# Hybrid SSD and attention block on one core: down-phase pools on other operands' places, output half by token tiles, meta keys of 128 rows

## The chip, the cores and the metric

One core of a Trainium2 chip. The metric is device time in microseconds for one execution of the whole kernel. The kernel before took 2267.64 us (median of three runs, 2267.42 to 2267.79).

## What is computed

One decoder layer over 1024 tokens of 1024 features, with 16 learned meta tokens ahead of them (L = 1040) which are dropped at the output. The reference, cut to what matters here:

```python
u = rms_norm(h, norm_mix_w)
z, xbc, dt, c_q, c_kv, k_rope, g_ssm, g_mla = split(u @ w_in)
y_ssm = ssd_mixer(...)                  # Mamba-2, chunks of 128
y_mla = mla_mixer(...)                  # 8 heads, causal, keys include the 16 meta tokens
    p = softmax(where(mask, s, -inf))
    o = einsum("bhqk,bkhv->bqhv", p, v)
mixed = sigmoid(g_ssm) * (y_ssm @ w_branch_ssm) + sigmoid(g_mla) * (y_mla @ w_branch_mla)
h = h + mixed @ w_out
v = rms_norm(h, norm_mlp_w)
h = h + square(relu(v @ w_mlp_up)) @ w_mlp_down
return rms_norm(h, final_norm_w)[:, 16:]
```

## The kernel before

Everything is float32. Each product is made of three matmuls on split operands: ACT casts a value to its high part (L69 from SBUF, L112 from PSUM), DVE subtracts that from the value to get the low part (L70, L113), and `mm` (L100) runs high x high, high x low and low x high. Weights come in units of 128 x 1024 (512 KB) by SP's DMA queue into tiles `st`, and their splits are the tiles `w`. Token tiles are 128 rows; the meta tokens are a ninth tile of 16 (`TILES` in the code, T and off being a tile's length and place). A scheduler with a simulated timeline sets the order of the instructions of each engine; the kernel text gives the dependences. SBUF pools are stacked from the left or the right side, so a pool that is opened later lies where closed ones lay, and its tiles wait for the last use of what lay there.

The program in the order of time: normalisation, transposes and the small key and dt projections (`pb`, L222 ff., `keys_and_dt`) for the nine token tiles; projections, convolution, gates and the SSD scan to 924 us; attention to 1254; branch products `pbr` and the output projection `pout` in two halves of 512 tokens to 1587; norms and transposes `tpv` to 1612; the MLP's up product to 1925 and its down product to 2252; the final norm.

Attention goes by head h (8) and block b of 256 queries. `probabilities` makes one 128-query row tile of softmaxed scores `pr`; `weighted_values` transposes them on PE (`pp`, L737), splits them into `pT` (L112, L113), and multiplies with the values `vt` to `po` (L100). Keys are taken in groups: first the 16 meta keys alone (kt = -1), then pairs of 128-key tiles. For the meta keys `pT` and `vt` have 16 rows, so each (h, b) issues three `po` of 16 rows, 96 in all; the other 480 have 128. `vt` holds nine key tiles for two heads (`values`, products `pv`), built once per head pair.

`out_half(t, mixed)` (L855 ff.) takes the two 512-column halves c of `w_out` one after the other; in each, all four token tiles' PSUM banks are filled in parallel over the eight k tiles, and only then DVE adds `pout` to `res` (L877). `row_norm` (L903 ff.) of a token tile needs both halves: squares on ACT (L911), their sum on DVE (L912), the power on POOL (L120), two scalings on DVE (L915). The up phase needs, for tokens 512 to 1023, `B22` and the four differences `T1` to `T4` (L941 to L947), each transposed on PE (`tpv`) and split; `B11` and `B21` come from the first half.

The MLP's two products each save an eighth of the block products (seven in place of eight per 2 x 2 block). Up: for each g of 8, seven products of 24 matmuls with `xT` or `xB` tiles (`xop`), from g = 1 on in the order B11, T1, T2, B22, T3, B21, T4; the hidden blocks go to DRAM (`d_h`, POOL's queue). Down: for each kb of 4, seven products of 48 matmuls from `h` (reloaded by `hid` as `hr` on SP's queue, L1091) and `w` (from `w_down`, slots `sd`, L963). Their results are added into the tiles `acc` (L1115), which POOL's queue has loaded from `d_res` (L1074, sixteen of 256 KB). `t1` is b12 - b11 first (L1119). In the profile `pm<-w,h` are the down matmuls, and the last product of each kb is the one of bank set `F`. After the last, `finish_row` runs `row_norm` per token tile and writes `out` (L1084).

## Time and profile before

| | us |
|---|---|
| median of three runs | 2267.64 |
| the profiled execution | 2268.88 |
| its span, first to last instruction | 2266.4 |
| PE busy | 2207.6 |
| DVE busy | 1371.3 |
| ACT busy | 1016.4 |
| POOL busy | 295.4 |

PE is TensorE's matmuls, PEld its weight loads, which run beside matmuls; DVE is VectorE, ACT ScalarE, POOL GpSimd, SP SyncE. A group's busy time counts overlapping instructions once. Where a row has "[x <-engine tile]", the engine sat idle x us before it, until that work was done. The mean granted TensorE clock of the span is 0.990 of full speed.

### The profile page before, as it was taken

To read this page: it belongs to the slowest core of one execution; us is meant where nothing else is said; L and a number is where in the kernel's file an instruction comes from. 1 tells how busy PE (TensorE), PEld (TensorE's weight loads), DVE (VectorE), ACT (ScalarE), POOL (GpSimd) and SP (SyncE) were. 2 spreads that over 40 slices of the span, in tenths; PEclk is the share of its full clock that TensorE was granted. 3 is DMA by queue.
4 is the path that set the end of the run, shared out by engine and by line. 5 is a ranking of instruction groups with operands and counts; after the bars stand their busy time and mean duration, and the time that the engine had idled before them with its cause. 6 is when DMAs were issued, how large, how long until landed. Compare 5 with 4: busy or idle time off the path is not lost.

```text
span 2266.4 us, 31520 instructions
## 1 busy us (share of the span) xinstructions
PE 2207.6 (97%) x12294; PEld 1934.0 (85%) x12294; DVE 1371.3 (61%) x2062; ACT 1016.4 (45%) x1824; POOL 295.4 (13%) x398
## 2 busy tenths in 40 slices
PE   7999999999999999999999999999899999699997
PEld 7999998999989988898888888888688887588886
DVE  6632468769769686356555333335764644777776
ACT  4432255646546454466665222232554545333333
POOL 2100002102112022000002121011021212100000
PEclk9999999999999999999999999999899999899999
DMA  6443454625526446522118686344344534854442
GB/s 191 103 99 89 103 147 131 149 62 162 126 85 159 97 139 160 200 57 64 54 47 256 204 278 223 111 126 135 102 164 134 172 116 154 292 167 140 149 121 84
DMA packets 238260, 314.57 MB, mean 139 GB/s; under 512 B 18576, under 2 KB 172048, under 8 KB 237600
## 3 DMA queue, kind: packets, MB, share of 16 engines
q1 hardware_dynamic: 148816, 201.31, 28.9%
q0 software_dynamic: 89296, 111.26, 17.8%
q8 instruction: 96, 1.57, 0.3%
q14 instruction: 52, 0.43, 0.1%
HBM read 221.11 MB, written 91.41 MB: 138 GB/s over the span
## 4 chain that ended last, share of the span: by engine, by line
PE 94%; DMA 3%; DVE 2%; ACT 1%; issue 1%; SPq 0%; POOL 0%; DVEq 0%; POOLq 0%; ACTq 0%
PE pm L100 26%; PE pg L100 16%; PE px L100 12%; PE pbr L100 11%; PE po L100 4%; PE pq L100 4%; PE pout L100 4%; PE sc L100 4%; PE pd L569 2%; PE pp L737 2%; PE pb L100 1%; PE pv L100 1%; DMA st<-in_w_down 1%; PE ps L100 1%; PE pr L100 1%; PE pk L100 1%
## 5 line engine op out<-in xcount | busy, mean ns | idle before, releaser
L70 DVE TENSOR_TENSOR w<-st,w 128x1024 fp32r<-128x1024 f32 x194 | 245.5, 1266 | 267.4 <-ACT w L69 266.4
L100 PE MATMUL pm<-w,h 128*128 128x512 f32 x1344 | 307.4, 391 | 19.4 <-ACT h L69 16.6
L100 PEld LDWEIGHTS pm<-w,h 128*128 128x128 f32 x1344 | 253.6, 189 | 73.2 <-ACT h L69 17.1
L69 ACT CAST w<-st 128x1024 fp32r<-128x1024 f32 x194 | 203.5, 1050 | 227.1 <-PE pbr L100 140.7
L100 PE MATMUL px<-uT,w 128*128 128x346 f32 (+1 forms) x1728 | 290.7, 323 | 0.0
L100 PEld LDWEIGHTS px<-uT,w 128*128 128x128 f32 x1728 | 275.6, 188 | 1.5
L100 PE MATMUL pbr<-ring,w 128*128 128x512 f32 x1152 | 264.8, 391 | 0.0
L100 PEld LDWEIGHTS pbr<-ring,w 128*128 128x128 f32 x1152 | 215.7, 188 | 45.9
L100 PE MATMUL pg<-w,uT 128*128 128x256 f32 x1536 | 195.8, 283 | 0.0
L100 PE MATMUL pg<-uT,w 128*128 128x512 f32 x768 | 194.3, 400 | 0.0
L100 PEld LDWEIGHTS pg<-w,uT 128*128 128x128 f32 x1536 | 188.1, 188 | 2.1 <-issue 0.4
L100 PE MATMUL pm<-xT,w 128*128 128x512 f32 x768 | 183.3, 395 | 0.0
L100 PEld LDWEIGHTS pm<-xT,w 128*128 128x128 f32 x768 | 144.0, 187 | 35.0
L100 PEld LDWEIGHTS pg<-uT,w 128*128 128x128 f32 x768 | 140.9, 188 | 30.7
L69 ACT CAST h<-hr 128x1024 fp32r<-128x1024 f32 x56 | 58.9, 1054 | 183.3 <-PE pm L100 172.2
L100 PE MATMUL pm<-xB,w 128*128 128x512 f32 x576 | 138.2, 396 | 1.6 <-ACT w L69 1.6
L100 PEld LDWEIGHTS pm<-xB,w 128*128 128x128 f32 x576 | 109.1, 190 | 26.9 <-ACT w L69 1.9
L419 DVE SCALAR_TENSOR_TENSOR xs<-raw,cw,xs 128x1040 f32<-128x1040 f32 x72 | 93.1, 1298 | 8.7 <-ACT xs L417 7.9
L511 ACT ACTIVATE m<-m,nacs 128x128 f32<-128x128 f32 x256 | 78.9, 390 | 39.5 <-DMA m<-d_acs 39.4
L100 PE MATMUL po<-pT,vt 128*128 128x256 f32 (+2 forms) x576 | 93.7, 291 | 1.6 <-ACT pT L112 0.7
L70 DVE TENSOR_TENSOR h<-hr,h 128x1024 fp32r<-128x1024 f32 x56 | 68.2, 1221 | 42.1 <-ACT h L69 42.1
L100 PE MATMUL pout<-w,mix 128*128 128x512 f32 x384 | 90.9, 396 | 0.0
(259 smaller groups left out, 3374.1 us busy)
## 6 DMA issues: line engine op xcount, KB each, us to landing
st<-in_w_in SPq DMA_DIRECT2D x60, 512.0 KB, 4.2
hr<-d_h SPq DMA_DIRECT2D x56, 512.0 KB, 3.6
m<-d_acs SPq DMA_DIRECT2D x32, 512.0 KB, 4.3
d_y<-yT POOLq DMA_DIRECT2D x32, 512.0 KB, 5.0
st<-in_w_bs SPq DMA_DIRECT2D x32, 512.0 KB, 3.6
ring<-d_y POOLq DMA_DIRECT2D x16, 1024.0 KB, 14.1
st<-in_w_up SPq DMA_DIRECT2D x32, 512.0 KB, 3.9
d_h<-hs POOLq DMA_DIRECT2D x64, 256.0 KB, 3.2
```

The source lines that it names most:

```text
L69: act.copy(out=hi, in_=src)
L70: dve.tensor_tensor(out=lo, in0=src, in1=f(hi), op=ALU.subtract)
L100: pe.matmul(out=out, lhsT=l, rhs=r, start=start, stop=stop, skip_group_check=more)
L419: dve.scalar_tensor_tensor(out=xs, in0=raw[:, k : k + L], scalar=cw[:, ct, k : k + 1], in1=xs, op0=ALU.mult, op1=ALU.add)
L511: act.activation(out=m[:, h, :], in_=m[:, h, :], func=AF.Relu, bias=nacs[:, i, hh])
L569: pe.matmul(out=pd[:, cs], lhsT=q["m"][:, h, :], rhs=q["xd"][:, cs], start=True, stop=True)
L737: pe.transpose(out=pt[:T, n : n + P], in_=prs[i - 2 * b][0][:, c0 : c0 + T], identity=ident)
```

## The change

1. `keys_and_dt`: the meta tile's products take 128 token columns as the stationary operand in place of 16 (the further ones belong to the next token tile and are not used).
2. Attention: the meta keys' `pT` becomes one of two permanent tiles `pTm` of 128 rows, zeroed once; slot 0 of `vt` is zeroed by POOL for each head pair, and the three `po` of the meta keys take all 128 rows.
3. The second output half becomes `out_rows`: token tiles outside, c inside; all eight units of `w_out` are held, those of c = 1 in a new pool `wop`.
4. `xop` is laid out in another order, and the down phase's pools move: `whl2` (for `h`) first and on the left, `sd` and `sh` on the right. `acc` becomes eight tiles of 128 x 1024, loaded by eight DMAs of 512 KB on POOL after the first product has been written down; `frow` comes there too.
5. The last product of the last kb runs by token tiles (`by_rows`); each `finish_row` writes one 512 KB output, on SP's queue for even and on ACT's for odd tiles.

```diff
@@ -224,10 +224,10 @@
             T, off = TILES[i]
             pb = pc.tile([P, 512], F32, tag="c", name="pb")
             for k in range(KD):
-                uh, ul = (uT[:, j, k, off : off + T] for j in (0, 1))
+                uh, ul = (uT[:, j, k, off : off + P] for j in (0, 1))
                 for w, us in ((0, uh), (1, uh), (0, ul)):
                     first, last = k == 0 and us is uh and w == 0, k == KD - 1 and us is ul
-                    mm(pb[:T, :352], us, t1w[:, k, w, :], first, last)
+                    mm(pb[:, :352], us, t1w[:, k, w, :], first, last)
             dve.tensor_copy(out=krr[:T, i, :], in_=pb[:T, 256:320])
             dve.tensor_tensor(out=dtr[:T, i, :], in0=pb[:T, 320:352], in1=dtb[:T], op=ALU.add)
             ckn = ap2.tile([P, 256], F32, tag="ckn", name="ckn", bufs=2)
@@ -636,6 +636,10 @@
         ckv = a0.tile([P, 2, 2, L], F32R, name="ckv")
         kr = a1.tile([P, 2, L], F32R, name="kr")
         causal = a1.tile([P, L], F32, name="causal")
+
+        metas = [a1.tile([P, 2, 256], F32R, name=f"pTm{j}") for j in range(2)]
+        for m in metas:
+            pool.memset(f(m), 0.0)
         pool.dma_start(out=cq, in_=d_cq)
         pool.dma_start(out=ckv, in_=d_ckv)
         pool.dma_start(out=kr, in_=d_kr)
@@ -650,6 +654,7 @@
         def values(wu, hh):
 
             vt = a1.tile([P, 2, 9, 2 * DV], F32R, tag="vt", name="vt")
+            pool.memset(f(vt[:, :, 0, :]), 0.0)
             for i, (T, off) in enumerate(TILES):
                 ps = pbank("pv")
                 out = ps[:T, : 2 * DV]
@@ -719,11 +724,11 @@
 
             out = pso.tile([P, 256], F32, tag="o", name="po")
             vs = slice(DV * hv, DV * (hv + 1))
-            def accumulate(T, pT, pieces):
+            def accumulate(pT, pieces):
                 for z, x in ((0, 0), (1, 0), (0, 1)):
                     for kt, p0, q0 in pieces:
-                        v = vt[:T, z, kt + 1, vs]
-                        mm(out[:, q0:], v, pT[:T, x, p0 : p0 + 256 - q0], kt < 0 and z == x, x == 1 and kt == 2 * b + 1)
+                        v = vt[:, z, kt + 1, vs]
+                        mm(out[:, q0:], v, pT[:, x, p0 : p0 + 256 - q0], kt < 0 and z == x, x == 1 and kt == 2 * b + 1)
 
             ready = []
             for g in [[-1]] + [[kt, kt + 1] for kt in range(0, 2 * b + 2, 2)]:
@@ -736,9 +741,9 @@
                     for i in range(i0, 2 * b + 2):
                         pe.transpose(out=pt[:T, n : n + P], in_=prs[i - 2 * b][0][:, c0 : c0 + T], identity=ident)
                         n += P
-                pT = a2.tile([P, 2, 512], F32R, tag="pT", name="pT", bufs=5)
+                pT = a2.tile([P, 2, 512], F32R, tag="pT", name="pT", bufs=5) if T == P else metas[b % 2]
                 split_psum(pT[:T, 0, :n], pT[:T, 1, :n], pt[:T, :n])
-                ready.append((T, pT, pieces))
+                ready.append((pT, pieces))
                 if len(ready) > PT_AHEAD:
                     accumulate(*ready.pop(0))
                 yield
@@ -876,6 +881,24 @@
                 sp.dma_start(out=dst, in_=a["x"][P * ti : P * (ti + 1), cs])
                 dve.tensor_tensor(out=dst, in0=dst, in1=ps[i], op=ALU.add)
 
+    def out_rows(t, mixed, pl):
+
+        wu = [[wunit(a["w_out"][2 * P * u : 2 * P * (u + 1), 512 * c : 512 * (c + 1)].rearrange("(k p) c -> p k c", p=P),
+                     (2, 512), (whl, pl)[c]) for u in range(4)] for c in range(2)]
+        for i in range(4):
+            ts = slice(P * i, P * (i + 1))
+            for c in range(2):
+                ps = pf.tile([P, 512], F32, tag="f", name="pout")
+                for k in range(8):
+                    wh, wl = (w[:, k % 2, :] for w in wu[c][k // 2])
+                    mm(ps, mixed[k][:, 0, ts], wh, k == 0, False)
+                    mm(ps, mixed[k][:, 0, ts], wl, False, False)
+                    mm(ps, mixed[k][:, 1, ts], wh, False, k == 7)
+                ti = 4 * t + i
+                dst = res[ti][c]
+                sp.dma_start(out=dst, in_=a["x"][P * ti : P * (ti + 1), 512 * c : 512 * (c + 1)])
+                dve.tensor_tensor(out=dst, in0=dst, in1=ps, op=ALU.add)
+
     out_half(0, mix_half(0))
     mixed = mix_half(1)
     ring_stack.close()
@@ -927,12 +950,13 @@
         row_norm(ep, i, row, True)
         transposed(xop["B11"], res[i][0], i)
         transposed(xop["B21"], res[i][1], i)
-    out_half(1, mixed)
+    with ExitStack() as ws:
+        out_rows(1, mixed, ws.enter_context(tc.tile_pool(name="wop", bufs=4, reuse_waits="tile")))
     br.close()
     with tc.using_default_side("right"):
         xb = ctx.enter_context(ExitStack())
         xbp = xb.enter_context(tc.tile_pool(name="xb", bufs=1, reuse_waits="tile"))
-    xop |= {n: xbp.tile([P, 2, 4, 512], F32R, name=f"x{n}") for n in ("B22", "T1", "T3", "T2", "T4")}
+    xop |= {n: xbp.tile([P, 2, 4, 512], F32R, name=f"x{n}") for n in ("T1", "T2", "B22", "T3", "T4")}
     for j in range(4):
         row_norm(ep, 4 + j, row, True)
         (b11, b21), (b12, b22) = res[j], res[4 + j]
@@ -1061,17 +1085,15 @@
     xb.close()
     xa_stack.close()
 
+    whl2 = ctx.enter_context(tc.tile_pool(name="whl2", bufs=4, reuse_waits="tile"))
     dn = ctx.enter_context(tc.tile_pool(name="dn", bufs=1, reuse_waits="tile"))
-    whl2 = ctx.enter_context(tc.tile_pool(name="whl2", bufs=4, reuse_waits="tile"))
-    sd = ctx.enter_context(tc.tile_pool(name="sd", bufs=10, reuse_waits="tile"))
-    sh = ctx.enter_context(tc.tile_pool(name="sh", bufs=4, reuse_waits="tile"))
     ef = ctx.enter_context(tc.tile_pool(name="ef", bufs=2, reuse_waits="tile"))
+    with tc.using_default_side("right"):
+        sd = ctx.enter_context(tc.tile_pool(name="sd", bufs=10, reuse_waits="tile"))
+        sh = ctx.enter_context(tc.tile_pool(name="sh", bufs=4, reuse_waits="tile"))
     row = dn.tile([P, D], F32, name="frow")
-    sp.dma_start(out=row, in_=a["fin_w"].partition_broadcast(P))
-    res = [[dn.tile([P, 512], F32, name=f"acc{i}{c}") for c in range(2)] for i in range(NT)]
-    for i in range(NT):
-        for c in range(2):
-            pool.dma_start(out=res[i][c], in_=d_res[:, i, 512 * c : 512 * (c + 1)])
+    acc = [dn.tile([P, D], F32, name=f"acc{i}") for i in range(NT)]
+    res = [[t[:, 512 * c : 512 * (c + 1)] for c in range(2)] for t in acc]
 
     def split_h(src):
         w = whl2.tile([P, 2, 1024], F32R, tag="w2", name="h")
@@ -1080,8 +1102,7 @@
 
     def finish_row(i):
         row_norm(ef, i, row, False)
-        for c in range(2):
-            sp.dma_start(out=a["out"][P * i : P * (i + 1), 512 * c : 512 * (c + 1)], in_=res[i][c])
+        (sp, act)[i % 2].dma_start(out=a["out"][P * i : P * (i + 1), :], in_=acc[i])
 
     for kb in range(4):
         subs = (2 * kb, 2 * kb + 1)
@@ -1097,17 +1118,27 @@
                 for g in subs
             ]
 
-        def product(out, n, w, start):
+        def product(out, n, w, start, by_rows=False):
+            hs, ws = [], []
+
+            def part(s, i):
+                ts = slice(P * i, P * (i + 1))
+                for k in range(2):
+                    hh, hl = hs[s][:, 0, k, ts], hs[s][:, 1, k, ts]
+                    mm(out[i], hh, ws[s][:, 0, k, :], start and s == k == 0, False, True)
+                    mm(out[i], hh, ws[s][:, 1, k, :], False, False, True)
+                    mm(out[i], hl, ws[s][:, 0, k, :], False, s == k == 1, True)
+
             for s, g in enumerate(subs):
-                hv = split_h(hid(n, g)).rearrange("p j (k c) -> p j k c", k=2)
-                wv = split_unit(w[s]).rearrange("p j (k c) -> p j k c", k=2)
-                for i, o in enumerate(out):
-                    ts = slice(P * i, P * (i + 1))
-                    for k in range(2):
-                        hh, hl = hv[:, 0, k, ts], hv[:, 1, k, ts]
-                        mm(o, hh, wv[:, 0, k, :], start and s == k == 0, False, True)
-                        mm(o, hh, wv[:, 1, k, :], False, False, True)
-                        mm(o, hl, wv[:, 0, k, :], False, s == k == 1, True)
+                hs.append(split_h(hid(n, g)).rearrange("p j (k c) -> p j k c", k=2))
+                ws.append(split_unit(w[s]).rearrange("p j (k c) -> p j k c", k=2))
+                if not by_rows:
+                    for i in range(4):
+                        part(s, i)
+            if by_rows:
+                for i in range(4):
+                    for s in range(2):
+                        part(s, i)
 
         def gather(src, half, c):
             for i, s in enumerate(src):
@@ -1123,6 +1154,10 @@
         combine(t1, b12, b11)
         E, G, F = ([bank() for _ in range(4)] for _ in range(3))
         product(G, 3, t1, True)
+        if kb == 0:
+            sp.dma_start(out=row, in_=a["fin_w"].partition_broadcast(P))
+            for i in (4, 5, 6, 7, 0, 1, 2, 3):
+                pool.dma_start(out=acc[i], in_=d_res[:, i, :])
         gather(G, 1, 1)
         b22 = rows(1, 1)
         product(G, 6, b22, False)
@@ -1139,7 +1174,7 @@
         combine(t1, b21, t1)
         product(E, 1, t1, False)
         gather(E, 1, 0)
-        product(F, 2, b21, True)
+        product(F, 2, b21, True, kb == 3)
         gather(F, 0, 0)
     for i in (4, 5, 6, 7, 0, 1, 2, 3):
         finish_row(i)
```

The rows below are from the built programs: line, operation, output<-inputs, shape, count. ACT from the last two copies of the up phase on, before (`t` is the difference t1; `w<-st` here are casts of w_down):

```order
L1006 ACTIVATE c_17479<-pm 128x512
L1007 ACTIVATE c_17479<-c_17479 128x512
L69 CAST w<-t_17575 128x1024
L69 CAST w<-t_17576 128x1024
L69 CAST w<-st 128x1024 x2
L69 CAST h<-hr 128x1024 x5
L69 CAST w<-st 128x1024
L69 CAST h<-hr 128x1024
L69 CAST w<-st 128x1024
L69 CAST h<-hr 128x1024
```

ACT at the same place now:

```order
L1030 ACTIVATE c_17459<-pm 128x512
L1031 ACTIVATE c_17459<-c_17459 128x512
L69 CAST w<-t_17530 128x1024
L69 CAST w<-t_17531 128x1024
L69 CAST h<-hr 128x1024 x4
L69 CAST w<-st 128x1024 x4
L69 CAST h<-hr 128x1024 x3
L69 CAST w<-t_17530 128x1024
L69 CAST h<-hr 128x1024
L69 CAST w<-t_17531 128x1024
```

Two `w<-st` stood between the casts of `t` and the first `h`; now four `h` come first and four `w<-st` behind them.

SP at the change from up to down, before:

```order
L1070 DMA frow<-in_fin_w 128x1024
L963 DMA st<-in_w_down 128x2x512 x4
L1091 DMA hr<-d_h 128x1024 x4
L963 DMA st<-in_w_down 128x2x512 x6
L1091 DMA hr<-d_h 128x1024 x5
L963 DMA st<-in_w_down 128x2x512
L1091 DMA hr<-d_h 128x1024
L963 DMA st<-in_w_down 128x2x512
```

and now:

```order
L987 DMA st<-in_w_down 128x2x512 x4
L1112 DMA hr<-d_h 128x1024 x4
L987 DMA st<-in_w_down 128x2x512 x4
L1112 DMA hr<-d_h 128x1024 x3
L1158 DMA frow<-in_fin_w 128x1024
L1112 DMA hr<-d_h 128x1024
L987 DMA st<-in_w_down 128x2x512 x4
L1112 DMA hr<-d_h 128x1024 x7
```

The first twelve loads are in the same order; `frow`, which stood ahead of all, now stands behind fifteen.

DVE from the add of the last `pout` on, before (`res_14719` is tile 3's second half; `res_14714` to `res_14717` are tiles 1 and 2, and another 35 rows follow up to the first `w<-st`):

```order
L877 TENSOR_TENSOR res_14719<-res_14719,pout 128x512
L119 TENSOR_SCALAR rv<-ss 128x1
L915 SCALAR_TENSOR_TENSOR res_14714<-res_14714,rv,row 128x512
L915 SCALAR_TENSOR_TENSOR res_14715<-res_14715,rv,row 128x512
L113 TENSOR_TENSOR xB_15092<-tpv,xB_15092 128x4x128
L941 TENSOR_TENSOR res<-res_14714,res 128x512
L912 TENSOR_TENSOR ss<-ss 128x1
L113 TENSOR_TENSOR xT_15093<-tpv,xT_15093 128x4x128
L915 SCALAR_TENSOR_TENSOR res_14716<-res_14716,rv,row 128x512
L915 SCALAR_TENSOR_TENSOR res_14717<-res_14717,rv,row 128x512
L113 TENSOR_TENSOR xT_15094<-tpv,xT_15094 128x4x128
L113 TENSOR_TENSOR xT_15095<-tpv,xT_15095 128x4x128
```

and now (`res_14695` is tile 3's second half, `res_14691` tile 1's):

```order
L900 TENSOR_TENSOR res_14695<-res_14695,pout 128x512
L113 TENSOR_TENSOR xB_15074<-tpv,xB_15074 128x4x128
L935 TENSOR_TENSOR ss<-ss 128x1
L969 TENSOR_TENSOR t_15143<-res_14691,res 128x512
L119 TENSOR_SCALAR rv<-ss 128x1
L113 TENSOR_TENSOR xT_15072<-tpv,xT_15072 128x4x128
L971 TENSOR_TENSOR res<-res,t_15143 128x512
L113 TENSOR_TENSOR xT_15075<-tpv,xT_15075 128x4x128
L113 TENSOR_TENSOR xT_15073<-tpv,xT_15073 128x4x128
L938 SCALAR_TENSOR_TENSOR res_14694<-res_14694,rv,row 128x512
L938 SCALAR_TENSOR_TENSOR res_14695<-res_14695,rv,row 128x512
L113 TENSOR_TENSOR xT_15076<-tpv,xT_15076 128x4x128
```

The scalings (STT with `row`) of tiles 1 and 2 no longer stand behind the last add, nor do four of the subtractions.

## Rows read from the trace of the kernel before

**Rows 1.** The page, busy time of each engine (share of the span, instructions).

```profile
PE 2207.6 (97%) x12294; PEld 1934.0 (85%) x12294; DVE 1371.3 (61%) x2062; ACT 1016.4 (45%) x1824; POOL 295.4 (13%) x398
```

**Rows 2.** Busy time by stage: window, length, PE, PEld, DVE, ACT, POOL, clock, DMA share, GB/s.

```profile
924.00:1254.00 330.00, 327.41 (x2143) 292.93 (x2142) 180.14 (x441) 202.10 (x427) 35.48 (x51) 1.00 0.34 98
1587.00:1612.00 25.00, 15.85 (x84) 12.36 (x84) 24.51 (x45) 13.54 (x26) 2.62 (x4) 0.80 0.40 126
1925.00:1942.00 17.00, 0.37 (x3) 0.09 (x1) 13.95 (x15) 6.49 (x8) 7.53 (x14) 0.63 1.03 396
```

**Rows 3.** Groups by form, attention (924 to 1254): busy, mean ns | idle before, releasers.

```profile
L100 PE MATMUL po<-pT,vt 128*128 128x256 f32 x384 | 70.0, 301 | 0.0
L100 PE MATMUL po<-pT,vt 16*128 16x256 f32 x96 | 22.4, 320 | 1.6 <-ACT pT L112 0.7
...
L100 PEld LDWEIGHTS po<-pT,vt 128*128 128x128 f32 x480 | 63.1, 189 | 3.5
L100 PEld LDWEIGHTS po<-pT,vt 16*128 16x128 f32 x96 | 14.0, 182 | 11.4 <-issue 6.2 <-ACT pT L112 4.2 <-DVE sm L714 0.9
```

**Rows 4.** Timeline of PE in attention: start, duration (us), line, operation, tile, count.

```profile
965.15 0.60 PE L737 MATMUL pp<-ident,pr 128*128 128x128 f32 x4
965.68 0.50 PE L100 MATMUL po<-pT,vt 16*128 16x256 f32 x2
...
1008.48 0.61 PE L100 MATMUL po<-pT,vt 16*128 16x256 f32 x3
1009.02 0.66 PE L737 MATMUL pp<-ident,pr 128*128 128x128 f32 x4
1009.43 0.95 PE L100 MATMUL po<-pT,vt 128*128 128x256 f32 x6
1010.22 0.49 PE L737 MATMUL pp<-ident,pr 128*128 128x128 f32 x3
1010.47 0.93 PE L100 MATMUL po<-pT,vt 128*128 128x256 f32 x6
```

**Rows 5.** DVE's groups from 1587.5 to 1611.8, and PE's timeline where they end.

```profile
L915 DVE SCALAR_TENSOR_TENSOR res<-res,rv,row 128x512 f32<-128x512 f32 x6 | 4.2, 746 | 0.0
L943 DVE TENSOR_TENSOR res<-res,res 128x512 f32<-128x512 f32 x3 | 2.1, 685 | 0.0
...
1611.70 8.24 PE L100 MATMUL pm<-xB,w 128*128 128x512 f32 x28 [1.62 <-ACT w L69]
```

**Rows 6.** Timeline from up to down, all engines (SPq is SP's DMA queue).

```profile
1908.63 7.10 SPq L963 DMA_DIRECT2D st<-in_w_down  x4
...
1919.52 5.77 PE L100 MATMUL pm<-xT,w 128*128 128x512 f32 x24
...
1929.98 2.18 ACT L69 CAST w<-t 128x1024 fp32r<-128x1024 f32 x2 [3.40 <-DVE t L1119]
...
1940.82 1.99 ACT L69 CAST h<-hr 128x1024 fp32r<-128x1024 f32 x2
...
1941.91 13.35 PE L100 MATMUL pm<-w,h 128*128 128x512 f32 x48 [16.63 <-ACT h L69]
...
1958.04 7.13 PE L100 MATMUL pm<-w,h 128*128 128x512 f32 x30 [2.79 <-ACT w L69]
```

**Rows 7.** DMA issues of 1900 to 1965, then of the whole run (page): us to landing last.

```profile
hr<-d_h SPq DMA_DIRECT2D x10, 512.0 KB, 9.9
...
hr<-d_h SPq DMA_DIRECT2D x56, 512.0 KB, 3.6
```

**Rows 8.** Timeline of the tail, PE and DVE.

```profile
2234.49 0.69 DVE L1115 TENSOR_TENSOR acc<-acc,pm 128x512 f32<-128x512 f32 x1
2234.74 17.39 PE L100 MATMUL pm<-w,h 128*128 128x512 f32 x76
...
2237.61 1.42 DVE L915 SCALAR_TENSOR_TENSOR acc<-acc,rv,frow 128x512 f32<-128x512 f32 x2 [0.68 <-POOL rv L120]
...
2258.07 1.41 DVE L915 SCALAR_TENSOR_TENSOR acc<-acc,rv,frow 128x512 f32<-128x512 f32 x2 [0.73 <-POOL rv L120]
```

## The prediction

> **What bounds the kernel.** I began with the page's busy times: TensorE (PE) works 2207.6 of 2266.4 us, 97% [rows 1]. A gain must come from time in which PE idles, or from matmuls that take longer than their columns ask. The table by stages shows three places [rows 2]. In attention (924 to 1254) PE is busy 327.41 of 330 us, ACT 202.10 and DVE 180.14, so only cheaper matmuls help there. From 1587 to 1612 PE is busy 15.85 of 25 us while DVE works 24.51: DVE is the bound. From 1925 to 1942 PE does nothing, DVE works 13.95 of 17 us and the DMA engines run at 396 GB/s. A fourth place is the tail after the last matmul [rows 8].
>
> The profiled execution took 2268.88 us for a span of 2266.4; the runs' median is 2267.64, 1.24 less. I sum on the profile and take 1.24 off. What this kernel's measurement can tell from no change is about 0.2%, 4.5 us.
>
> **1. Meta tile at the start (pb): 0.** The 24 matmuls stream the same 352 columns; they now load 128 instead of 16 stationary columns and also wait for the next token tile's split. Loads run beside matmuls elsewhere (the 480 full po loads idle 3.5 us in all [rows 3]), so I take 0, with 0.5 lost as the bad end; below 0 nothing is left out.
>
> **2. Attention: 96 matmuls of 16 rows become 128 rows; about -12 us.** One profile row hides the price: 96 short po take 22.4 us, 0.233 each, 384 full ones 70.0, 0.182 each [rows 3], but overlapping records are merged in these. Starts are cleaner [rows 4]. Three 16-row matmuls from 1008.48 to 1009.02: 0.18 each; six full ones from 1009.43 to 1010.22: 0.13. That is 0.05 per matmul, 96 x 0.05 = 4.8 us, the lower end. Around them more is lost. Three transposes (pp) ahead of a full po take 0.25 us, 0.083 each (1010.22 to 1010.47); four ahead of a 16-row po take 0.53 (965.15 to 965.68), 0.20 more than 4 x 0.083; four behind one take 0.41 (1009.02 to 1009.43), 0.08 more. It looks as if PE drained where the row count changes: the weight loads of the 96 show 11.4 us of idle ahead of them, those of the 480 full ones 3.5 [rows 3]. The timeline of the stage has the 96 in 43 groups, so 43 x 0.28 = 12.0, with the 4.8 16.8 us, the upper end. I take 12: PE is the stage's bound, but a part of each entry is a wait for ACT's copy of pT that stays.
>
> The Trainium skill speaks against this part: "TensorE: Matmul & The Clock Gate", section "Why this matters for your kernels", says that a single matmul of K=32 takes the time of one with K=128. By it the padding is worth nothing. The rows differ, 0.18 against 0.13 [rows 4], and I go by them; the rule has its place among the rivals.
>
> What is added: a memset of a 128x512 piece per head pair on POOL, three of which wait for the previous pair's last po. POOL is busy 35.48 of 330 us [rows 2], and the other eight tiles of V are split meanwhile: 0. If that cover failed it would be under 1 us each, 3 in all.
>
> **3. Last output half by token tiles: -5 us.** Before, all four token tiles end together, and DVE works from the last pout to 1611.70, where the first up matmul starts [rows 5]. In that window it has 6 scalings, 3 each of the four subtractions, and 20 splits. By DVE's new order only tile 3's share stays behind the last pout: 2 scalings, 8 subtractions, the same 20 splits, since all 80 transposes still follow the last pout on PE. So 4 x 0.746 and 4 x 0.685 [rows 5] go, 5.7 us; starts overlap a little, so I take 5. It would be 1 if PE's transposes and ACT's copies become late instead, 6 at best. The order of pout costs PE its c = 1 weights earlier: all eight units must be cast; the first token tile's c = 0 work (24 matmuls) covers that, and I put a loss of up to 1.5 us into the lower end, which is then -0.5.
>
> **4. Up to down: -6 us, the least certain.** Before, the last up matmul ends at 1919.52 + 5.77 = 1925.29 and the first down matmul starts at 1941.91 after 16.63 us of idle "<-ACT h"; another 2.79 us are lost at 1958.04 [rows 6]. The differences t are cast from 1929.98 to 1932.16, and the first h only at 1940.82 [rows 6]: ACT's order has two casts of b22 in between, which wait for their loads. In the new order h stands directly behind the two t casts, and b22 after four h. That wait, 1932.16 to 1940.82, 8.7 us, goes.
>
> But something is late next. The new slots of w_down lie on the right: the first on B22's place, the next on T4's. In the built program the second load's wait for PE is that for T4's last matmul, 1925.29; the three other first weights, and all hr loads behind them in SP's queue, start there rather than from 1908.63 on [rows 6]. So for these slots "released first" doesn't hold. A load then takes between 3.6 us (hr's median over the run) and 9.9 (the median in this crowded stretch) [rows 7]. Behind it come t (about two of the 0.685 subtractions [rows 5], 1.3) and three casts, two of t and one of h, 1.09 each (2.18 for two [rows 6]): 4.6, about 4.5 as DVE and ACT overlap. First down matmul between 1925.3 + 3.6 + 4.5 = 1933.4 and 1925.3 + 9.9 + 4.5 = 1939.7; I take 1937, a gain of 4.9, since POOL's acc loads, which stood ahead of eight of the d_h writes, now stand behind them and leave the first loads some room. Of the second stall I take half, 1.4. Together 6. The ends: +11 gained (1933.4, no second stall); 3 lost, if four weights, four hr and POOL's eight writes, 6.3 MB, end together: 6.3/0.396 = 15.9 us, 1941.2 + 3.7 = 1945.
>
> **5. The tail: -2 us.** Before, the last matmul ends at 2234.74 + 17.39 = 2252.13 and DVE's last scaling at 2258.07 + 1.41 = 2259.48: 7.35 us, because several row tiles finish together [rows 8]. With the last product by rows one tile is left; a lone tile takes from its add at 2234.49 to its scaling's end at 2237.61 + 1.42 = 2239.03, 4.5, plus 0.2 from PE to DVE: a gain of 2.6. One 512 KB output in place of two of 256 KB may cost some of it; the trace has no such row at the end. Range 0 to 3; I take 2.
>
> **Sum:** 0 + 12 + 5 + 6 + 2 = 25 us; 2268.88 - 25 - 1.24 = 2242.6, say **2243**. The ends added up: 4.8 - 0.5 - 3 + 0 - 0.5 = 0.8 and 16.8 + 6 + 11 + 3 = 36.8. All at one end is unlikely; a gain of 12 to 35 covers the forecast's own case, 2232 to 2256.
>
> **The rivals.**
> - *Padding gives nothing*: if the 0.05, 0.20 and 0.08 belong to the chain through ACT's pT copies and not to the row count, part 2 falls to 0 and 25 becomes 13: 2268.88 - 13 - 1.24 = 2254.6. For it: the meta tile's pT is the first of its block, so a wait for ACT would show there above all. Against it: inside a run of three, where everything has arrived, the 16-row ones still take 0.18 and the full ones 0.13 [rows 4]. It is also what the Trainium skill's rule above would give. Chance 0.13.
> - *The pools don't do what the title says*: T4's slots make the first matmul come at 1945 and the second stall stays or grows by 2: part 4 turns from -6 to +5, the sum is 14, time 2253.6. For it: 396 GB/s is already the stretch's rate [rows 2]. Against it: the waits ahead of h are gone. Chance 0.11.
> - *Slower:* the DMA engines share everything that is outstanding, so that the first needed load ends with the last. After 1925.3 SP has 15 loads of 512 KB in its order before it waits, 7.9 MB, and frow 0.5; POOL's writes and acc loads are 6.3 MB. 14.7 MB at 396 GB/s are 37 us: 1962.4 + 4.5 = 1966.9, 25 us later than 1941.91, while the other parts give 19: 2268.88 + 6 - 1.24 = 2273.6. It decides from a first matmul later than about 1965 (1941.9 + 19 + 4.5). For it: transfers in the crowded stretch take 9.9 us, not 3.6 [rows 7]. Against it: even there a load ended in 9.9, not 37. Chance 0.04.
> - The forecast's case: 0.72.
>
> **How the numbers follow.** The time is that of the forecast's case. The two faster rivals lie inside its upper end; to hold the time 8 times in 10 I reach from 2231 to 2258. Faster by over 0.2% (under 2263): the forecast and nearly all of the two rivals beside it, 0.92. Slower (over 2272): 0.03 of the slow rival's 0.04. Within: the rest, 0.05, cases in which the lower ends of several parts meet.
>
> **What would show it.** In attention: po all of 128 rows, PE's busy time there down by about 12 us, pp ahead of a meta po at 0.083 each. First pm at about 19 us behind the last pout, not 24. SP's second w_down load when T4's last matmul ends, the first down matmul some 12 us behind T4, not 16.6. From the last matmul to the last scaling about 5 us. Wrong would be: the attention stage as long as before with new waits on ACT pT, or the first down matmul later than 16.6 us behind T4.

## The result, and the profile after

The changed kernel takes 2253.19 us (median of four runs, 2251.38 to 2254.46) against 2267.53 before: ratio 0.9937, 95% interval 0.9919 to 0.9954. That is 14.3 us less; 24.6 were forecast (2267.64 to 2243). A second reading (last experiment) gave 2253.55, ratio 0.9936. The profiled execution has a span of 2250.9 us, 15.5 less than the 2266.4 of before. The page's busy times of the changed kernel, to be read against [rows 1]:

```profile
PE 2191.1 (97%) x12294; PEld 1932.1 (86%) x12294; DVE 1371.8 (61%) x2062; ACT 1017.9 (45%) x1824; POOL 293.5 (13%) x396
```

PE works 16.5 us less, though it runs the same 12294 matmuls. To see where, I follow PE's timeline at the borders of the stages: the first matmul of attention, a block of meta keys, the first output matmul of the second half, the first up matmul, the last block of T4, and the first two stretches of down (columns: start, duration, line, operation, tile, count, idle before). The changed kernel:

```profile
922.86 5.63 PE L100 MATMUL pq<-cq,w 128*128 128x512 f32 x24
...
1003.42 0.61 PE L100 MATMUL po<-pTm,vt 128*128 128x256 f32 x3
1003.87 0.60 PE L742 MATMUL pp<-ident,pr 128*128 128x128 f32 x4
...
1523.84 2.72 PE L100 MATMUL pout<-w,mix 128*128 128x512 f32 x11
...
1592.43 8.23 PE L100 MATMUL pm<-xB,w 128*128 128x512 f32 x28 [1.62 <-ACT w L69]
...
1900.24 5.77 PE L100 MATMUL pm<-xT,w 128*128 128x512 f32 x24
1920.85 12.54 PE L100 MATMUL pm<-w,h 128*128 128x512 f32 x48 [14.85 <-ACT h L69]
1942.28 27.96 PE L100 MATMUL pm<-w,h 128*128 128x512 f32 x111 [8.90 <-ACT h L69]
```

The kernel before at three borders that [rows 5] and [rows 6] don't hold (its last `pout` ends at 1552.91 + 34.77, with 1587.5 the next matmul's start):

```profile
924.17 5.63 PE L100 MATMUL pq<-cq,w 128*128 128x512 f32 x24
...
1538.49 2.72 PE L100 MATMUL pout<-w,mix 128*128 128x512 f32 x11
...
1552.91 34.77 PE L100 MATMUL pout<-w,mix 128*128 128x512 f32 x148
```

| from | to | before | after | change |
|---|---|---|---|---|
| start | first `pq` of attention | 924.17 | 922.86 | -1.3 |
| there | first `pout` of the second half | 614.32 | 600.98 | -13.3 |
| there | first up matmul | 73.21 | 68.59 | -4.6 |
| there | last T4 block's end (start + duration) | 313.59 | 313.58 | 0 |
| there | second stretch of down | 32.75 | 36.27 | +3.5 |
| there | last matmul's end | 294.09 | 296.57 | +2.5 |
| there | span's end | 14.27 | 12.05 | -2.2 |

They add up to the span's -15.5, but for rounding. Attention and the output half gave what was forecast, the tail too. From up to down 6 us were forecast as gained and 6 were lost. That place in the changed kernel, all engines:

```profile
1889.40 18.17 SPq L987 DMA_DIRECT2D st<-in_w_down  x4
...
1907.68 2.96 SPq L1112 DMA_DIRECT2D hr<-d_h  x4
...
1914.07 1.23 DVE L1150 TENSOR_TENSOR t<-st 128x1024 f32<-128x1024 f32 x1 [5.45 <-DMA st<-in_w_down]
...
1919.44 3.66 POOL L1160 DMA_DIRECT2D acc<-d_res  x7 [8.53 <-DMA d_h<-hs]
1919.75 1.05 ACT L69 CAST h<-hr 128x1024 fp32r<-128x1024 f32 x1
...
1922.23 4.55 SPq L1112 DMA_DIRECT2D hr<-d_h  x3
...
1925.86 1.05 ACT L69 CAST h<-hr 128x1024 fp32r<-128x1024 f32 x1 [1.35 <-DMA hr<-d_h]
...
1941.18 1.05 ACT L69 CAST h<-hr 128x1024 fp32r<-128x1024 f32 x1 [4.88 <-DMA hr<-d_h]
```

SP's row of four `st` lasts 18.17 us: it sends the first at 1889.40 and is held until T4's last matmul ends at 1900.24 + 5.77 = 1906.01; the four `hr` follow at 1907.68. The first t comes at 1914.07, the first h cast at 1919.75, PE starts at 1920.85, 14.85 us behind T4 (16.63 before). Then the fifth `hr`, sent at 1922.23, lands 18.9 us later; ACT casts it at 1941.18, and PE, done with its first 48 matmuls at 1933.39, waits 8.90 us (2.79 before). The DMA issues of the same stretch (KB each, median us to landing):

```profile
hr<-d_h SPq DMA_DIRECT2D x10, 512.0 KB, 14.9
```

An `hr` took 14.9 us, against 9.9 and 3.6 in [rows 7]; the eight acc loads beside them took 11.7.

That PE waits for the fifth `h` also comes from its own order. The first 48 matmuls are one product and use two of the four `h` that are cast by 1926.91; the other two belong to b22's product, whose first weights are split by 1933.18, when PE is about to come free. But in the built program the product of b11, with the fifth and sixth `h`, stands second in PE's order and b22's third. In the kernel before and in all the variants of the down phase below, too, the fifth `h` is wanted ahead of the third; the last of them takes b11 first of all. No run here put b22's product second, so what that would save isn't shown.

After the stall the granted clock is lower for a while (its mean over the two levels of 1.2 and 2.4 GHz; columns as in [rows 2], the clock third from the end):

```profile
1942.00:1952.00 10.00, 9.72 (x32) 7.79 (x33) 5.19 (x7) 2.71 (x4) 0.00 (x0) 0.72 1.01 386
```

0.72 from 1942 to 1952. The 111 matmuls from 1942.28 on take 27.96 us, 0.252 each; where the stall is short (the opposite order, below) 160 take 36.57, 0.229 each. Over 111 that is 2.6 us, the 2.5 lost behind the stall.

The tail:

```profile
2214.66 24.19 PE L100 MATMUL pm<-w,h 128*128 128x512 f32 x106
...
2239.55 0.68 DVE L1146 TENSOR_TENSOR acc<-acc,pm 128x512 f32<-128x512 f32 x1
...
2243.42 1.41 DVE L938 SCALAR_TENSOR_TENSOR acc<-acc,rv,frow 128x512 f32<-128x512 f32 x2 [0.73 <-POOL rv L120]
```

The last matmul ends at 2214.66 + 24.19 = 2238.85, the last scaling at 2243.42 + 1.41 = 2244.83: 5.98 us where [rows 8] give 7.35. From there to the span's end it is 6.1 us, before 6.9.

### The profile page after: what moved, and what is told of

Same layout as the page of the kernel before. It is cut to its first block, busy times and chain, and to the rows that moved or that the text cites. A ratio compares the mean times of both kernels' runs of the same rounds, so it can differ in the third digit from the quotient of the medians.

```text
span 2250.9 us, 31476 instructions
## 1 busy us (share of the span) xinstructions
PE 2191.1 (97%) x12294; PEld 1932.1 (86%) x12294; DVE 1371.8 (61%) x2062; ACT 1017.9 (45%) x1824; POOL 293.5 (13%) x396
## 4 chain that ended last, share of the span: by engine, by line
PE 94%; DMA 2%; DVE 2%; ACT 1%; issue 1%; SPq 0%; POOL 0%; DVEq 0%; POOLq 0%; ACTq 0%
PE pm L100 27%; PE pg L100 16%; PE px L100 12%; PE pbr L100 11%; PE po L100 4%; PE pq L100 4%; PE pout L100 4%; PE sc L100 4%; PE pd L569 2%; PE pp L742 2%; PE pb L100 1%; PE pv L100 1%; PE ps L100 1%; PE pr L100 1%; PE pk L100 1%; DMA hr<-d_h 1%
## 5 line engine op out<-in xcount | busy, mean ns | idle before, releaser
L100 PEld LDWEIGHTS pm<-w,h 128*128 128x128 f32 x1344 | 255.0, 190 | 77.9 <-ACT h L69 24.6
L100 PEld LDWEIGHTS pout<-w,mix 128*128 128x128 f32 x384 | 71.7, 188 | 17.3 <-DVE w L70 0.4
```

The lines of the kernel that those rows point to most:

```text
L100: pe.matmul(out=out, lhsT=l, rhs=r, start=start, stop=stop, skip_group_check=more)
```

## The experiments

### Attention's padding alone

The kernel before with part 2 of the change alone (two zeroed tiles `pTm`, the zeroed slot of `vt`, all rows in `accumulate`).

```diff
+            pool.memset(f(vt[:, :, 0, :]), 0.0)
...
-                pT = a2.tile([P, 2, 512], F32R, tag="pT", name="pT", bufs=5)
+                pT = a2.tile([P, 2, 512], F32R, tag="pT", name="pT", bufs=5) if T == P else metas[b % 2]
...
-                ready.append((T, pT, pieces))
+                ready.append((T if T == P else P, pT, pieces))
```

> The kernel before with the padding of the meta keys in attention alone. My theory (a matmul of 16 rows between matmuls of 128 rows costs the drain at each change of the row count): 12 to 14 us less, 2254 to 2256. Rival (a matmul of few rows takes as long as one of 128, and the gain of the stage in the changed kernel comes from elsewhere): within 2 us of 2267.5.

Measured: 2255.24 us, ratio 0.9949 (0.9932 to 0.9966), 11.7 us less. PE's timeline:

```profile
922.88 5.63 PE L100 MATMUL pq<-cq,w 128*128 128x512 f32 x24
...
1524.00 2.72 PE L100 MATMUL pout<-w,mix 128*128 128x512 f32 x11
```

From the first `pq` to the first `pout` of the second half 601.12 us, as in the changed kernel (600.98), 13.2 less than before. The rival falls.

### The same, padded to 64 rows

```diff
-                        v = vt[:T, z, kt + 1, vs]
+                        v = vt[:K, z, kt + 1, vs]
...
-                ready.append((T, pT, pieces))
+                ready.append((T if T == P else 64, pT, pieces))
```

> The kernel before with the meta keys of attention padded to 64 rows only, not 128. My theory (what costs is that the row count changes between neighbours on TensorE, whatever it is): a gain of 0 to 4 us of the 12, 2263 to 2267. Rival (what costs is the small row count itself): most of the gain is there, 2255 to 2260.

Measured: 2269.45 us, ratio 1.0003 (0.9994 to 1.0012): nothing gained of the 0 to 4 us that were forecast (the kernel before took 2268.51 beside it), and the rival falls. PE's timeline, the borders and one block of meta keys:

```profile
922.85 2.45 PE L100 MATMUL pq<-cq,w 128*128 128x512 f32 x10
...
1007.07 0.61 PE L100 MATMUL po<-pTm,vt 64*128 64x256 f32 x3
1007.61 0.66 PE L742 MATMUL pp<-ident,pr 128*128 128x128 f32 x4
...
1537.39 2.72 PE L100 MATMUL pout<-w,mix 128*128 128x512 f32 x11
```

The stage lasts 1537.39 - 922.85 = 614.54 us, before 614.32. Three `po` of 64 rows take 0.54 us up to the next transposes (1007.07 to 1007.61), as three of 16 rows do in [rows 4] (1008.48 to 1009.02); three of 128 rows in the changed kernel take 0.45 (1003.42 to 1003.87).

Where in a run of three the price lies shows when its matmuls are looked at one by one: first the second with the third, then the third alone (windows of the timeline that hold no more), and the transposes ahead of a run. The kernel before, the one with 64 rows and the changed kernel:

```profile
1008.67 0.41 PE L100 MATMUL po<-pT,vt 16*128 16x256 f32 x2
1008.79 0.30 PE L100 MATMUL po<-pT,vt 16*128 16x256 f32 x1
...
1007.39 0.29 PE L100 MATMUL po<-pTm,vt 64*128 64x256 f32 x1
...
962.59 0.60 PE L742 MATMUL pp<-ident,pr 128*128 128x128 f32 x4
962.95 0.49 PE L100 MATMUL po<-pTm,vt 128*128 128x256 f32 x2
...
1003.61 0.42 PE L100 MATMUL po<-pTm,vt 128*128 128x256 f32 x2
1003.73 0.30 PE L100 MATMUL po<-pTm,vt 128*128 128x256 f32 x1
```

The third starts 0.12 us behind the second with 16 rows and with 128 alike. The step out of the run differs: from the start of the third to that of the next transposes it is 0.23 us with 16 rows (1008.79 to 1009.02), 0.22 with 64 (1007.39 to 1007.61) and 0.14 with 128 (1003.73 to 1003.87). So does the step in: four transposes ahead of the run take 0.53 us in [rows 4] (965.15 to 965.68) and 0.36 in the changed kernel (962.59 to 962.95). So the price belongs to the change of the row count, not to the count of 16.

### The output half by token tiles alone

The kernel before with `out_rows` (as in the change) in place of the second `out_half`.

```diff
-    out_half(1, mixed)
+    with ExitStack() as ws:
+        out_rows(1, mixed, ws.enter_context(tc.tile_pool(name="wop", bufs=4, reuse_waits="tile")))
```

> The kernel before with the second output half by token tiles alone. My theory (DVE has less behind the last output matmul): first up matmul 19 to 20 us behind the last output matmul in place of 24, time 4 to 5 us less, 2263. Rival (the end moves but the weights of the second column half, wanted earlier, hold PE at the start of the half): the two cancel, 2266 to 2268.

Measured: 2262.74 us, ratio 0.9982 (0.9972 to 0.9991), 4.2 us less. PE's timeline:

```profile
1538.73 2.72 PE L100 MATMUL pout<-w,mix 128*128 128x512 f32 x11
...
1556.01 32.50 PE L100 MATMUL pout<-w,mix 128*128 128x512 f32 x138
...
1607.88 7.00 PE L100 MATMUL pm<-xB,w 128*128 128x512 f32 x28 [1.62 <-ACT w L69]
```

The half's matmuls begin at 1538.73, the last ends just before 1588.4 (1556.01 + 32.50 = 1588.51, with the next transposes at 1588.34), so they hold PE 49.6 us, before 49.0; the first up matmul comes at 1607.88, 19.5 us behind, before 24.2. The rival's mechanism costs 0.6 us, not 5.

### The opposite order of the up operands

```diff
-    ("T1", "T2", "B22", "T3", "T4")
+    ("T4", "T3", "B22", "T2", "T1")
```

The down phase's ten weight slots keep their addresses; under them now lie half of B22, T2 and T1, and T4 lies under none. The edit moves more than that: two of the four `hr` slots lie on T3 in place of T2, and T4 lies under the last `acc` tile.

> The changed kernel with the up operands declared in the opposite order, so that the first ten weight slots of the down phase lie on T1, T2 and half of B22, and none on T4. Theory A (the three weights and the h loads that wait behind T4's last matmul are what keeps the first down matmul 14.85 us behind T4 and makes the second stall of 8.9 us): the loads start some 15 us earlier, the first down matmul comes 2 to 6 us behind T4, the second stall is under 4, the time 2253 falls to 2233 to 2240. Theory B (the DMA engines are simply full with what has to be moved there, 17.6 MB in 65 us, and only the amount counts): the first matmul comes a little earlier, the stall behind it grows, and the time falls by 5 us at most, to 2248 or more.

Measured: 2237.87 us, ratio 0.9872 (0.9858 to 0.9887), 29 us less than before and 15 less than the changed kernel. PE's timeline behind the last T4 block:

```profile
1913.14 13.44 PE L100 MATMUL pm<-w,h 128*128 128x512 f32 x48 [7.98 <-ACT h L69]
1928.67 36.57 PE L100 MATMUL pm<-w,h 128*128 128x512 f32 x160 [2.08 <-ACT h L69]
```

The first down matmul comes 7.98 us behind T4 (forecast 2 to 6, 14.85 in the changed kernel), the second stall is 2.08 us (8.90). Theory B falls: the same bytes are moved, the three held loads only 17 us earlier. What holds the remaining 8 us stands in the timeline of all engines:

```profile
1888.56 1.91 SPq L987 DMA_DIRECT2D st<-in_w_down  x4
...
1907.50 1.29 DVE L1083 TENSOR_TENSOR hs<-c,hs 128x512 f32<-128x512 f32 x2 [0.41 <-DMA d_h<-c]
...
1908.71 2.35 DVE L1150 TENSOR_TENSOR t<-st 128x1024 f32<-128x1024 f32 x2
```

SP sends all four weights from 1888.56 on, within 1.91 us. The differences t start at 1908.71 right behind DVE's last sums of the up phase (`hs`), which waited 0.41 us for a d_h write. So what comes next is DVE's order, not a load of w or h; but these sums had themselves been held by d_h writes, 3.07 us at 1903.36 and 0.41 at 1904.47, so waits for transfers are not out of it.

### Four acc loads on SP's queue

```diff
-            for i in (4, 5, 6, 7, 0, 1, 2, 3):
+            for i in (4, 5, 6, 7):
                 pool.dma_start(out=acc[i], in_=d_res[:, i, :])
...
         product(G, 6, b22, False)
+        product(E, 0, b11, True)
+        if kb == 0:
+            for i in (0, 1, 2, 3):
+                sp.dma_start(out=acc[i], in_=d_res[:, i, :])
         gather(G, 0, 1)
-        product(E, 0, b11, True)
```

The edit also moves b11's product ahead of `gather(G, 0, 1)` in the text; in PE's order it stood second already.

> The changed kernel with four of the eight acc loads (2.1 MB) taken off POOL's queue and put on SP's behind the first seven h loads. Theory A: the first down matmul stays 14 to 15 us behind T4; the second stall shrinks by what 2.1 MB take at 400 GB/s, 5 us, if the loads were what held the fifth h load; the time is 2248 to 2253. Theory B: the stall of 8.9 us goes altogether and the time falls to 2244 or less.

Measured: 2247.4 us, ratio 0.9909 (0.9894 to 0.9924). PE's timeline behind the last T4 block:

```profile
1922.18 13.96 PE L100 MATMUL pm<-w,h 128*128 128x512 f32 x48 [15.17 <-ACT h L69]
1938.22 27.05 PE L100 MATMUL pm<-w,h 128*128 128x512 f32 x111 [2.09 <-ACT h L69]
```

The first matmul stays 15.17 us behind T4, the second stall shrinks to 2.09. The time lies just outside what theory A gave and well above what B gave: given PE's order of products, the stall goes with two things, loads that start late and acc loads that share the engines with them; either one removed takes most of it away, but only the first one moves the start.

### The pools back where they were

The changed kernel with the up operands and the pools `dn`, `whl2`, `sd`, `sh`, `ef` as in the kernel before.

```diff
-    ("T1", "T2", "B22", "T3", "T4")
+    ("B22", "T1", "T3", "T2", "T4")
...
+    dn = ctx.enter_context(tc.tile_pool(name="dn", bufs=1, reuse_waits="tile"))
     whl2 = ctx.enter_context(tc.tile_pool(name="whl2", bufs=4, reuse_waits="tile"))
-    dn = ctx.enter_context(tc.tile_pool(name="dn", bufs=1, reuse_waits="tile"))
+    sd = ctx.enter_context(tc.tile_pool(name="sd", bufs=10, reuse_waits="tile"))
+    sh = ctx.enter_context(tc.tile_pool(name="sh", bufs=4, reuse_waits="tile"))
     ef = ctx.enter_context(tc.tile_pool(name="ef", bufs=2, reuse_waits="tile"))
-    with tc.using_default_side("right"):
-        sd = ctx.enter_context(tc.tile_pool(name="sd", bufs=10, reuse_waits="tile"))
-        sh = ctx.enter_context(tc.tile_pool(name="sh", bufs=4, reuse_waits="tile"))
```

> The changed kernel with the down phase's pools and the up operands back where they were before, all else kept (acc still eight tiles of 512 KB, asked for in the same place of the program). Theory A (the place of the pools costs time): the first three weights wait for B22 and T3 again, not T4; the first down matmul comes 10 to 14 us behind T4, the stall behind it is 5 or less, time 2242 to 2249. Theory B (the place does not matter, the amount to be moved does): first matmul and second stall add up to the 24 us of the changed kernel, time 2251 to 2255.

Measured: 2249.54 us, ratio 0.9913 (0.9898 to 0.9928), some 4 us less than the changed kernel. PE's timeline behind the last T4 block:

```profile
1921.11 12.63 PE L100 MATMUL pm<-w,h 128*128 128x512 f32 x48 [12.87 <-ACT h L69]
1940.61 29.69 PE L100 MATMUL pm<-w,h 128*128 128x512 f32 x121 [6.88 <-ACT w L69]
```

The first matmul is 12.87 us behind T4, but the stall is 6.88, more than theory A allowed, and the time lies between what the two theories gave: in this build the scheduler puts POOL's acc loads ahead of the last d_h writes again (from 1902.92 on). From T4's end (1902.46 + 5.77 = 1908.23) to the second stretch it is 32.38 us: the changed kernel has 36.27, the kernel before 32.75. So the pools' new place, together with the order that it brings, lost about 4 us there (the two were not separated); without it the stretch is what it was, 0.4 less.

### The opposite order and the four acc loads together

Both edits, as shown above, in one kernel.

> The changed kernel with both the opposite order of the up operands and four of the acc loads on SP's queue. Theory A: in the first of the two the loads no longer set the start, DVE's order does (the differences t stand behind the last sums of the up phase), so the second edit adds little: 2235 to 2239, second stall 0 to 2. Theory B (bytes): 2.1 MB less ahead of the h loads take another 5 us: 2233 or less.

Measured: 2238.08 us, ratio 0.9866 (0.9851 to 0.988). By PE's idle times the start is 8.05 us behind T4 and the stall 2.08, as with the opposite order alone (7.98 and 2.08): with the loads early, the acc loads no longer matter. Theory A holds.

### The last product in the old order

```diff
-        product(F, 2, b21, True, kb == 3)
+        product(F, 2, b21, True)
```

> The changed kernel with the very last product in the old order, unit by unit, and not by token tiles; the outputs stay one transfer of 512 KB per token tile. My theory (the last product by rows leaves one tile behind the last matmul): the last scaling comes about 7.4 us behind the last matmul in place of 6.0, time 2254 to 2256. Rival (the tail's gain comes from the single 512 KB output on two queues): time unchanged, 2253.

Measured: 2254.92 us, ratio 0.9938 (0.9921 to 0.9954), which by itself can't be told from the changed kernel. The timeline of PE and DVE can:

```profile
2214.75 25.09 PE L100 MATMUL pm<-w,h 128*128 128x512 f32 x110
...
2245.79 1.41 DVE L938 SCALAR_TENSOR_TENSOR acc<-acc,rv,frow 128x512 f32<-128x512 f32 x2 [0.73 <-POOL rv L120]
```

The last matmul ends at 2239.84, the last scaling at 2247.20: 7.36 us, as before the change, against 5.98. From there to the span's end (2253.2) it is 6.0. So by_rows gives 1.4 us. The remaining 0.8 of the tail goes with the outputs of 512 KB on two queues, which both builds have; which of the two it is wasn't tried.

### The first product without a difference

The opposite order, with b11's product first, and its h loads asked for ahead of the weights:

```diff
-        b12, b11 = rows(0, 1), rows(0, 0)
+        h0 = [hid(0, g) for g in subs]
+        b11 = rows(0, 0)
+        h3 = [hid(3, g) for g in subs]
+        b12 = rows(0, 1)
...
-        product(G, 3, t1, True)
+        product(E, 0, b11, True, hr=h0)
...
-            for i in (4, 5, 6, 7, 0, 1, 2, 3):
+            for i in (0, 1, 2, 3, 4, 5, 6, 7):
...
+        gather(E, 0, 0)
+        product(G, 3, t1, True, hr=h3)
         gather(G, 1, 1)
...
         gather(G, 0, 1)
-        product(E, 0, b11, True)
-        gather(E, 0, 0)
```

> The changed kernel with the up operands in the opposite order, the first down product taken as that of b11 (which needs no difference t), its h loads asked for first and its weights next. My theory (once nothing waits for T4, the differences t behind DVE's last sums of the up phase hold the first matmul 8 us behind T4): the first down matmul comes 4 to 6 us behind T4, the stall behind it stays under 4, time 2231 to 2236, 2 to 6 less than with the opposite order alone. Rival (the full DMA queues set the start): first matmul 7 us or more behind T4, or a stall that takes the gain back, time 2237 or more.

Measured: 2244.23 us, ratio 0.9897 (0.9882 to 0.9912), 6 us more than the opposite order alone. PE's timeline behind the last T4 block, and DVE's ahead of the second row's end of waiting:

```profile
1909.68 2.08 PE L100 MATMUL pm<-w,h 128*128 128x512 f32 x4 [4.18 <-ACT w L69]
...
1943.92 66.33 PE L100 MATMUL pm<-w,h 128*128 128x512 f32 x281 [7.34 <-DVE acc L1146]
...
1941.96 1.22 DVE L1150 TENSOR_TENSOR t<-st,t 128x1024 f32<-128x1024 f32 x1
1943.09 0.68 DVE L1146 TENSOR_TENSOR acc<-acc,pm 128x512 f32<-128x512 f32 x1
```

The start is 4.18 us behind T4, as hoped, and the rival's other half came true: a stall of 7.34 us two products later. The gather that PE waits for is DVE's add at 1943.09, and it stands in DVE's order behind a t at 1941.96 and the differences with b22, two of which waited for its loads (1.60 us at 1929.68, 0.47 at 1934.00). A start that is 3.8 us earlier only reaches the next wait sooner.

### The changed kernel again

No edit.

> The changed kernel again, on the same chip as the run beside it, for a second reading of what it gains: 13 to 16 us less than before.

Measured: 2253.55 us (2251.11 to 2254.56), ratio 0.9936 (0.992 to 0.9953), 14.5 us less than before.

## Why the prediction was right, and where it was not

The time lies in the range of 2231 to 2258, but 10 us above the 2243 that were forecast. Parts 1, 2, 3 and 5 came within 1.5 us each; part 4 had the wrong sign. The range held because it had been drawn wide enough to take in the rival that came true, and that is no merit of part 4.

- **Part 1 (meta tile at the start, 0):** the stage before attention is 1.3 us shorter, but the two builds with padded attention and an unpadded `pb` start attention at 922.88 and 922.85, the changed kernel at 922.86. Two builds with the padded `pb` start it at 925.53 and 925.67 (the old pools, the old last product). So it is no effect of the padding. Taken as 0, right.
- **Part 2 (attention, -12):** -13.3 in the changed kernel, -13.2 alone. Right in size, and in the mechanism behind "43 x 0.28", a price where the row count changes. The other reading, that inside a run of three the 16-row matmuls take 0.18 and the full ones 0.13, was wrong: 0.18 is an average with the step out in it, and the third starts 0.12 us behind the second with 16 rows as with 128. The Trainium skill ("TensorE: Matmul & The Clock Gate", "Why this matters for your kernels") says that a single matmul of K=32 takes as long as one of K=128. Inside a run the trace agrees, 0.12 us with 16 rows and with 128; what three `po` lose, 0.54 us with 16 or 64 rows against 0.45 with 128, lies at the change. My sign for it, "PE's busy time there down", was a bad one: in a fixed window of 330 us PE is as busy as before (326.90 us, 327.41 before), because the stage is shorter; the borders show it.
- **Part 3 (output half, -5):** -4.6 in the changed kernel, 4.2 in the runs of the part alone. In the trace DVE's scalings in the stretch behind the last `pout` went from the six of [rows 5] to two, as the order said.
- **Part 4 (up to down, -6): wrong.** +3.5 up to the second stretch and +2.5 behind it. The wait for T4 was named, and the first matmul came 14.85 us behind T4, inside the bounds (8.1 to 19.7 by the forecast's ends) though 3 later than taken. The step that failed is "Of the second stall I take half, 1.4": it was 8.90. I had the late start delay only the first product. But PE takes b11's product second, with the fifth and sixth h. "SP has 15 loads in its order before it waits" was misread: there are four slots for `hr`, so after twelve loads SP waits until the first is split, at 1922.23. The fifth `hr` then runs beside 4.2 MB of acc loads, which the change put behind the last d_h writes (seven of the eight from 1919.44 on), and takes 18.9 us. The median was 14.9, where my upper bound was 9.9, a number from a stretch in which five of the acc loads, of half the size, had been sent ahead, at 1919.84. The lower clock after the stall, 2.5 us, was in no term. The lower end also added 3.7 us behind the loads where the sum has 4.5.
- **Part 5 (tail, -2):** -2.2; 1.4 from the last product by rows (2.6 forecast; the last add starts at 2239.55, 0.7 behind the last matmul, as DVE is busy with other tiles' scalings), 0.8 with the outputs.
- **The rivals.** "The pools don't do what the title says" is what happened, at 0.11: it gave 2253.6. It was right on the sum and the cause, T4's place, not on the shape: the start came 1.8 us sooner than before (14.85 behind T4, not 19.7), and the stall grew by 6.1, not by 2. "Padding gives nothing" gave 2254.6 and is refuted, though the time alone could not have told the two apart; the stages did.

The fastest version here is the changed kernel with the opposite order of the up operands: 2237.87 us, 29 less than before.

## What to carry to other kernels

When a pool is laid over released tiles, list for each new slot, in the order in which they are filled, which tile lies there and when that tile's last use ends; here one late tile under the second slot held the whole queue of loads for 16 us. When a wait is removed at a stage's start, follow the loads of the second and third step too, with everything that is moved behind the same instant, and read in the order of the waiting engine which load it will want next. Where matmuls of few rows alternate with full ones, as the 96 here, the changes of the row count cost time, and padding with zeros to the full count is worth trying.

## What was not expected of the hardware

The 24 `pb` matmuls of the third token tile run the same code in both of these builds, the kernel before (first) and the kernel with attention padded. Of each PE's timeline and the table by stretch, columns as in [rows 2]:

```profile
27.88 5.67 PE L100 MATMUL pb<-t1w,uT 128*128 128x352 f32 x24
...
28.00:33.00 5.00, 5.00 (x24) 5.00 (x23) 3.58 (x8) 1.85 (x4) 2.01 (x3) 0.66 0.69 174
```

```profile
28.06 4.13 PE L100 MATMUL pb<-t1w,uT 128*128 128x352 f32 x24
...
28.00:33.00 5.00, 5.00 (x34) 5.00 (x33) 4.09 (x10) 2.36 (x6) 2.01 (x3) 1.00 0.67 179
```

5.67 us and 4.13, at a mean granted clock of 0.66 and 1.00 from 28 to 33. From 10 to 28 both have 1.00, so it isn't that the full clock comes later: it is taken back once. The profiled executions of four builds show this fall (before, the output half alone, the old pools, the old last product), and these four start attention between 924.17 and 925.67, all others between 922.85 and 923.69; so the 1.3 us at the first border go with it. What sets it off stays open: from 22 to 28 PE was busy 3.77 us in the kernel before and 3.65 in the changed kernel, which kept 1.00. And padding by a factor of four, to 64 rows, brought nothing; the gain came whole at 128.
